# The last row block of a hybrid decoder layer: one group of 512 columns, and a bias that waits in the output

## The chip, the core and the metric

The kernel runs on one core of one Trainium2 chip. A core has TensorE (matrix products into PSUM), VectorE, ScalarE, GpSimd and SyncE, each with its own queue of instructions, and 16 DMA engines that all queues share. The metric is the device time of one execution in microseconds; the time before is the median of three runs.

## The reference

One decoder layer on 512 tokens of width 1024: two token mixers (a gated MLP and a differential attention) are projected, gated and merged, and the result goes through one more projection, a residual sum and a LayerNorm. What matters here is its end, cut to this:

```python
merged = jax.nn.sigmoid(ga) * (ya @ w_branch_a[i]) + jax.nn.sigmoid(gb) * (yb @ w_branch_b[i])
mix_out = merged @ w_out[i]
ple = jax.nn.sigmoid(x @ w_ple_gate[i]) * (p[i] @ w_ple[i])
x = layer_norm(DEEPNORM_ALPHA * x + mix_out + ple, ln_g[i], ln_b[i])
```

`layer_norm` takes mean and variance of each token's 1024 values, and returns (value - mean) * (variance + 1e-5)^-0.5 * ln_g + ln_b, in float32.

## The kernel before, in words

Every product is made of three passes (`three`): each float32 operand is split into a high and a low part, and high x high, high x low and low x high are added up in PSUM. `product` issues one pass and counts it; work on other engines is written out by hand with `later(n, ...)`, which puts a call n passes ahead, so that its instructions enter their engines' queues at that place. Each engine works through its queue in order. Tile semaphores are set by the framework; instructions wait only for what they read or overwrite.

The final projection works on four row blocks of 128 tokens (t = 0 to 3) and 1024 columns. A PSUM bank holds 128 x 512 float32. The first half of the columns (0 to 511) is done for row blocks 0 and 1 together, then 2 and 3; the second half row block by row block, t = 0 to 3, 8 slices of the contraction with three passes each. Before its products, a bank is filled by ScalarE (`fill`, L1321) with what is to be added: the gated embedding, and for the last row block also the residual, so that for t = 3 the finished sum stands in PSUM. For t < 3 the residual is added by VectorE in `stats` (L1338), into the SBUF tile `base`.

For the last row block alone, the second half is cut into two groups of 256 columns (`last_columns`, L1318), each in a bank of its own: 24 passes of 256 columns into a bank of tag `sc`, then 24 into one of tag `pp`. The statistics of the first group (`bn_stats`, L1341) run while TensorE does the second.

`last_norm` (L1343) normalizes a row block. `rstd_of` (L1091) lets VectorE aggregate the statistics (L1093) and add epsilon to the variance (L1094), and GpSimd raise it to the power -0.5 (L1096). Meanwhile VectorE centres: it subtracts the mean and multiplies by `ln_g` (L1351), for t = 3 straight from PSUM in three operations of 512, 256 and 256 columns. Then it scales by the power and adds `ln_b` (L1355), for t = 3 in two halves, and SyncE stores each half as it is finished (L1356).

Two queues matter beside these. SyncE issues the loads of the weights and, behind them, the stores of the output; its queue is empty between the last load and the first store. GpSimd issues the transfers that add to their destination (L324, L365, L1246). The last of them adds x to `base` for the last row block; behind it, in `later(RETIRE, pool.drain)` (L1382), GpSimd is told to drain. When all is issued, the program's end (L1435) drains each engine and lets them meet.

Of the kernel before, what the change touches and what calls it, by code (L numbers as in the profile page):

```python
# [17 lines left out]
AF = mybir.ActivationFunctionType  # L18
OP = mybir.AluOpType
AX = mybir.AxisListType  # L20

P = 128
D = 1024
T = 512
KT = D // P
NT = T // P
# [4 lines left out]
ALPHA = 2.0 ** 0.25  # L31
LAM_INIT = 0.2
EPS = 1e-5
# [52 lines left out]
MERGE = (36, 36, 25, 27), (40, 40, 68, 62)  # L86
RESIDUE = (176, 190, 204, 164)
FIRST_FILL = (150, 156)
FILL = ((14, 0, 1), (20, 2, 0), (24, 1, 1), (44, 3, 0), (110, 2, 1), (124, 3, 1), (150, 3, 2))
RETIRE = 8  # L90

# [135 lines left out]
def bcast(ap, n, parts=P):  # L229
    return bass.AP(tensor=ap.tensor, offset=ap.offset, ap=[[0, parts], [1, n]])  # L230
# [3 lines left out]
def hybrid_layer(ctx: ExitStack, tc: tile.TileContext, a, out: bass.AP):  # L234
    nc = tc.nc
    pe, dve, act, pool, sp = nc.tensor, nc.vector, nc.scalar, nc.gpsimd, nc.sync
# [12 lines left out]
    def pp():  # L249
        return pbank("pp", 3)  # L250
# [11 lines left out]
    def later(n, fn, *args):  # L262

        clock[1] += 1
        heapq.heappush(agenda, (clock[0] + n, clock[1], fn, args))

    def product(ps, s, m, start, stop, read_within=False):
        pe.matmul(ps, s, m, start=start, stop=stop, skip_group_check=read_within)  # L268
        clock[0] += 1
        while agenda and agenda[0][0] <= clock[0]:  # L270
            _, _, fn, args = heapq.heappop(agenda)
            fn(*args)
# [6 lines left out]
    def three(ps, s_h, s_l, m_h, m_l, first, last, read_within=False):  # L279

        product(ps, s_h, m_h, first, False, read_within)
        product(ps, s_h, m_l, False, False, read_within)
        product(ps, s_l, m_h, False, last, read_within)
# [3 lines left out]
    raw, split = {}, {}  # L287
    cursor = [0]

    def cut(h, l, x, alone=False):  # L290
        if alone:
            dve.tensor_copy(h, x)
        else:
            act.activation(h, x, AF.Copy)  # L294
        dve.tensor_tensor(out=l, in0=x, in1=h.bitcast(F32), op=OP.subtract)  # L295
# [37 lines left out]
    def load(u, cuts=(0, 1024), first=(sp,)):  # L333
        if u >= len(STEPS) or u in raw or STEPS[u][3] is not None:
            return
        _, unit, chain, _ = STEPS[u]
        if pumping:
            if not free:
                return
            home[u] = free.popleft()  # L340
            r = home[u]()
        elif chain == "a":
            r = sums[0]()
        else:
            ring.rotate(-1)
            home[u] = ring[-1]
            r = home[u]()
        raw[u] = r
        for j, s in enumerate(map(slice, cuts, cuts[1:])):
            queue = first[j] if j < len(first) else sp  # L350
            queue.dma_start(out=r[:, s], in_=weights(unit)[:, s])
            yield

    def follow(u):

        if u not in FOLLOWS:
            back = home.pop(u, None)
            if pumping and back:
                free.append(back)
                pump()  # L360
        else:
            raw[FOLLOWS[u]] = raw[u]
            if u in home:
                home[FOLLOWS[u]] = home.pop(u)
            pool.dma_start(out=raw[u], in_=weights(STEPS[FOLLOWS[u]][1]), accum_op=OP.add)  # L365

    def parts_of(u):
        h = wsp.tile([P, 1024], F32R, name="wh", tag="wh")
        l = wsp.tile([P, 1024], F32R, name="wl", tag="wl")
        split[u] = (h, l)  # L370
        return h, l

    def prep(u, cuts=(0, 1024)):
        if u < len(STEPS) and u not in split:
            run(load(u))
            h, l = parts_of(u)
            for s in map(slice, cuts, cuts[1:]):
                cut(h[:, s], l[:, s], raw[u][:, s])
                yield
            follow(u)  # L380
# [17 lines left out]
    def next_unit(name):  # L398
        u = cursor[0]
        assert STEPS[u][0] == name, (STEPS[u][0], name)  # L400
        cursor[0] += 1
        for g in (prep(u), prep(u + 1), prep(u + 2)):
            run(g)
        if not pumping:
            for v in range(u + 3, u + 6):
                run(load(v))
        spread(u + 3)
        if name in EARLY_ASK:
            later(ASK, lambda: run(load(u + 6)))
        return split.pop(u)  # L410
# [27 lines left out]
    def run(gen):  # L438
        for _ in gen:
            pass  # L440
# [24 lines left out]
    xh = big.tile([P, KT, T], F32R, name="xh", tag="X0")  # L465
    xl = big.tile([P, KT, T], F32R, name="xl", tag="X1")
# [6 lines left out]
    def ask_xr(k):  # L473
# [14 lines left out]
                       base=0, pattern=[[-1, P]], channel_multiplier=1)  # L488
    mhalf = consts.tile([P, 8], F32, name="mhalf")
# [4 lines left out]
    cs = rp.tile([P, T], F32, name="cs")  # L494
# [12 lines left out]
    def small(shape, name, bufs=6):  # L507
        return consts.tile(shape, F32, name=name, tag=name, bufs=bufs)
# [62 lines left out]
    cuts = [prep(u, halves) for u in range(3)]  # L571
# [43 lines left out]
    def of_sum(parts, c):  # L615
        def at(t, k):
            ts = slice(0, 2 * P) if t is None else slice(t * P, (t + 1) * P)
            return parts[0][:, c, k, ts], parts[1][:, c, k, ts]

        return at  # L620
# [313 lines left out]
    for k in range(KT):  # L934
        if k % 2 == 0:
            h, l = next_unit("kq")
# [93 lines left out]
    for g in range(KT):  # L1030
        bank = pp()
# [59 lines left out]
    def rstd_of(st):  # L1091
        mv = small([P, 2], "mv")
        dve.bn_aggr(out=mv, in_=st)  # L1093
        dve.tensor_scalar(out=mv[:, 1:2], in0=mv[:, 1:2], scalar1=EPS, scalar2=None, op0=OP.add)  # L1094
        rs = small([P, 1], "rs")
        pool.tensor_tensor(out=rs, in0=mv[:, 1:2], in1=mhalf[:, 0:1], op=OP.pow)  # L1096
        return mv, rs
# [110 lines left out]
    base = post.tile([P, NT, D], F32, name="base", tag="V")  # L1208
# [44 lines left out]
    for c in (1, 0):  # L1253
        h, l = next_unit("ple")
        for t in range(NT):
            ts = slice(t * P, (t + 1) * P)
            for k in range(2):
                m = slice(k * T, (k + 1) * T)
# [33 lines left out]
    norm_last = []  # L1292
# [13 lines left out]
    def merge_turn(c, t, m):  # L1306
        bank = pbank("tr" if t % 2 else "po", 1)
        for j in range(4):
# [6 lines left out]

    of_ya = (of_parts(xh, xl, 0, 0), of_parts(xh, xl, 4, 0), of_parts(xh, xl, 4, 2 * P),
             of_sum(ys, 2), of_sum(ys, 1), of_sum(ys, 0), of_apart)
    last_columns = [[(0, T), (T, D)] for _ in range(NT - 1)] + [[(0, T), (T, T + T // 2), (T + T // 2, D)]]  # L1318
    held = {}

    def fill(t, i):  # L1321
        c0, c1 = last_columns[t][i]
        bank = (pbank("sc", 2) if (t < 2 and i == 0) or (t >= 2 and i == 1) else
                pbank("tx", 1) if t == 2 else pp())
        held[t, i] = bank[:, :c1 - c0]
        act.activation(held[t, i], base[:, t, c0:c1], AF.Copy, scale=1.0 if t < NT - 1 else ALPHA)

    for t in range(2):
        later(FIRST_FILL[t], fill, t, 0)
# [10 lines left out]
            bank = z  # L1340
        dve.bn_stats(out=zst[t][:, piece, :], in_=bank)  # L1341

    def last_norm(t, cuts):  # L1343
        mv, rs = rstd_of(zst[t])
        lg, lb = norm_last
        if t < NT - 1:
            first = [(base[:, t, :], slice(0, D))]
        else:
            first = [(held[t, i], slice(*c)) for i, c in enumerate(last_columns[t])]
        for source, cs in first:  # L1350
            dve.scalar_tensor_tensor(out=base[:, t, cs], in0=source, scalar=mv[:, 0:1], in1=lg[:, cs],  # L1351
                                     op0=OP.subtract, op1=OP.mult)
        for cs in cuts:
            z = base[:, t, cs]
            dve.scalar_tensor_tensor(out=z, in0=z, scalar=rs[:, 0:1], in1=lb[:, cs], op0=OP.mult, op1=OP.add)  # L1355
            sp.dma_start(out=out[t * P:(t + 1) * P, cs], in_=z)  # L1356

    zst = [small([P, 2 if t < NT - 1 else 3, 6], "vst", 4) for t in range(NT)]
    units = []
    for n, t, i in FILL:  # L1360
        later(n, fill, t, i)
    for those in ((0, 1), (2, 3)):
        for k in range(KT):
# [9 lines left out]
            h, l = units[k // 2]  # L1373
            m = slice((k % 2) * T, (k % 2 + 1) * T)
            for t in those:
                ts = slice(t * P, (t + 1) * P)
# [4 lines left out]
    spread(cursor[0] + 3, *OUT_SECOND)  # L1381
    later(RETIRE, pool.drain)  # L1382
    units = []
    for t in range(NT):
        ts = slice(t * P, (t + 1) * P)
        for i, (c0, c1) in enumerate(last_columns[t][1:], 1):
            for k in range(KT):
                if len(units) <= k // 2:
                    run(prep(cursor[0]))
                    units.append(split.pop(cursor[0]))  # L1390
                    cursor[0] += 1
                h, l = units[k // 2]
                m = slice((k % 2) * T + c0 - T, (k % 2) * T + c1 - T)
                three(held[t, i], xh[:, k, ts], xl[:, k, ts], h[:, m], l[:, m], False, k == KT - 1, True)
            later(1, stats, t, i, held[t, i])
        later(1, last_norm, t, [slice(0, D)] if t < NT - 1 else [slice(0, T), slice(T, D)])
    flush()


# [39 lines left out]
```

## Time and profile before

| | us |
|---|---|
| median of 3 runs (lowest, highest) | 611.57 (611.23, 611.86) |
| the profiled execution | 611.03 |
| its span, first to last instruction | 609.3 |
| TensorE busy | 601.1 (99%) |
| VectorE busy | 466.3 (77%) |
| ScalarE busy | 345.9 (57%) |
| GpSimd busy | 125.1 (21%) |

The profile is one execution, and its times are counted from the start of its span. PE is TensorE, DVE VectorE, ACT ScalarE, POOL GpSimd and SP SyncE; a "q" behind the name means the engine's queue of issued instructions, such as DMA issues and drains. L and a number is the line of the kernel. The chain of work that ended last is followed back from the last instruction, at each step to what released it. The granted clock of TensorE was 0.996 of full speed.

### The profile page before, as it was taken

What the parts mean: (1) busy time and instruction counts of PE and PEld (TensorE: products, weight loads), DVE (VectorE), ACT (ScalarE), POOL (GpSimd) and SP (SyncE); (2) the same over time, 40 slices, a digit from 0 to 9 for tenths busy, and PEclk for the clock granted to TensorE, in tenths of its full rate; (3) what the DMA queues carried; (4) which work ended last, traced back from release to release, by engine and by line L of the source; (5) the groups of instructions that cost most, each with busy time, mean ns of one, the idle gap of its engine ahead of it and who ended that gap; (6) DMA issues with size and microseconds to landing.
All of it is one profiled execution on the core that took longest, in us unless ns stands there. A gap on an engine that the chain in (4) does not pass through costs nothing.

```text
span 609.3 us, 8273 instructions
## 1 busy us (share of the span) xinstructions
PE 601.1 (99%) x2880; PEld 501.9 (82%) x2880; DVE 466.3 (77%) x770; ACT 345.9 (57%) x537; POOL 125.1 (21%) x133
## 2 busy tenths in 40 slices
PE   9999999999999999999999999999999999999995
PEld 6888888888888888888888888888888888888885
DVE  6995645588789789777966779779687887879476
ACT  6656475754745745747576666554776565555310
POOL 1234121040350530520211322331120011110011
PEclk9999999999999999999999999999999999999998
DMA  8689899696886996893479988976999578998002
GB/s 307 226 248 183 251 206 224 238 252 237 276 196 249 308 248 243 220 317 108 118 305 294 291 245 215 267 186 185 287 242 312 173 202 251 239 248 308 31 35 103
DMA packets 44541, 138.23 MB, mean 227 GB/s; under 512 B 5940, under 2 KB 7092, under 8 KB 44148
## 3 DMA queue, kind: packets, MB, share of 16 engines
q1 hardware_dynamic: 34436, 102.97, 47.0%
q0 software_dynamic: 9488, 34.35, 30.8%
q8 instruction: 22, 0.36, 0.2%
q10 hardware_dynamic: 576, 0.39, 0.2%
q14 instruction: 19, 0.16, 0.1%
HBM read 118.69 MB, written 29.49 MB: 243 GB/s over the span
## 4 chain that ended last, share of the span: by engine, by line
PE 98%; DVE 1%; DMA 1%; DVEq 0%; issue 0%
PE ps_pp L268 56%; PE ps_sc L268 22%; PE ps_tx L268 9%; PE ps_sc L770 3%; PE ps_po L815 3%; PE ps_tr L804 1%; PE ps_po L268 1%; PE ps_tr L268 1%; PE ps_tr L1123 1%; PE ps_po L1123 1%; DMA xr<-in_xT 1%; PE ps_tx L858 1%; PE ps_tr L1309 0%; PE ps_po L1309 0%; DVE base L1351 0%; DVE xl L295 0%
## 5 line engine op out<-in xcount | busy, mean ns | idle before, releaser
L392 DVE TENSOR_TENSOR wl<-wr,wh 128x1024 fp32r<-128x1024 f32 x133 | 166.4, 1259 | 39.8 <-ACT wh L389 39.7
L389 ACT ACTIVATE wh<-wr 128x1024 fp32r<-128x1024 f32 x133 | 139.2, 1054 | 73.3 <-PE ps_pp L268 18.0
L268 PE MATMUL ps_pp<-xh,wh 128*128 128x512 f32 x232 | 94.0, 406 | 0.0
L268 PE MATMUL ps_pp<-xl,wh 128*128 128x512 f32 x232 | 92.7, 400 | 0.2 <-DVE xl L295 0.2
L268 PE MATMUL ps_pp<-xh,wl 128*128 128x512 f32 x232 | 91.8, 396 | 0.0
L783 ACT ACTIVATE p<-p,sth 128x128 f32<-128x128 f32 (+3 forms) x64 | 35.5, 556 | 41.1 <-DVE sth L781 41.1
L365 POOL DMA_DIRECT2D wr<-in_w x30 | 25.8, 873 | 155.8 <-DVE wl L392 152.8
L268 PE MATMUL ps_pp<-wl,xh 128*128 128x512 f32 (+1 forms) x148 | 56.9, 384 | 0.0
L268 PE MATMUL ps_pp<-wh,xl 128*128 128x512 f32 (+1 forms) x148 | 56.8, 384 | 0.0
L268 PE MATMUL ps_pp<-wh,xh 128*128 128x512 f32 (+1 forms) x148 | 56.7, 383 | 0.0
L268 PEld LDWEIGHTS ps_pp<-xl,wh 128*128 128x128 f32 x232 | 43.7, 188 | 7.9 <-DVE xl L295 0.5
L268 PEld LDWEIGHTS ps_pp<-xh,wh 128*128 128x128 f32 x232 | 43.7, 188 | 7.9 <-ACT wh L294 0.5
L268 PEld LDWEIGHTS ps_pp<-xh,wl 128*128 128x128 f32 x232 | 43.7, 188 | 7.7
L777 DVE CUSTOM_DVE_ANT_0 p<-ps_sc,mask 128x128 f32<-128x128 f32 (+3 forms) x64 | 31.0, 484 | 12.3 <-PE ps_sc L770 12.1
L715 POOL TENSOR_TENSOR hl<-m,hl 128x512 fp32r<-128x512 f32 x16 | 24.7, 1585 | 56.4 <-ACT hl L710 54.9
L268 PE MATMUL ps_sc<-wl,xsh 128*128 128x512 f32 x88 | 34.5, 392 | 0.0
L268 PE MATMUL ps_sc<-wh,xsh 128*128 128x512 f32 x88 | 34.4, 390 | 0.0
L268 PE MATMUL ps_sc<-wh,xsl 128*128 128x512 f32 x88 | 34.3, 390 | 0.0
L268 PEld LDWEIGHTS ps_pp<-wh,xh 128*128 128x128 f32 x148 | 27.8, 188 | 5.5
L268 PEld LDWEIGHTS ps_pp<-wl,xh 128*128 128x128 f32 x148 | 27.8, 188 | 5.4
L268 PEld LDWEIGHTS ps_pp<-wh,xl 128*128 128x128 f32 x148 | 27.8, 188 | 5.4
L268 PE MATMUL ps_pp<-wh,xsl 128*128 128x512 f32 x72 | 28.1, 390 | 0.0
(304 smaller groups left out, 1317.8 us busy)
## 6 DMA issues: line engine op xcount, KB each, us to landing
wr<-in_w SPq DMA_DIRECT2D x83, 512.0 KB, 5.4
wr<-in_w POOLq DMA_DIRECT2D x30, 512.0 KB, 7.2
wa<-in_w POOLq DMA_DIRECT2D x12, 512.0 KB, 6.5
k<-hl SPq DMA_DIRECT2D x16, 256.0 KB, 4.7
q<-hl SPq DMA_DIRECT2D x16, 256.0 KB, 4.3
ws_va<-in_w POOLq DMA_DIRECT2D x8, 512.0 KB, 9.8
wr<-ws_va SPq DMA_DIRECT2D x8, 512.0 KB, 4.8
kx<-hl SPq DMA_DIRECT2D x12, 256.0 KB, 6.3
```

What stands on the lines that cost most here:

```text
L268: pe.matmul(ps, s, m, start=start, stop=stop, skip_group_check=read_within)
L365: pool.dma_start(out=raw[u], in_=weights(STEPS[FOLLOWS[u]][1]), accum_op=OP.add)
L389: act.activation(h, raw[u], AF.Copy)
L392: dve.tensor_tensor(out=l, in0=raw[u], in1=h.bitcast(F32), op=OP.subtract)
L715: pool.tensor_tensor(out=hl[:, 3 - j, :], in0=m[2 * j], in1=hl[:, j, :].bitcast(F32), op=OP.subtract)
L770: pe.matmul(sc[m][:, :n], q[:, m, i * P:(i + 1) * P], kk[:, m, :n], start=o == 0, stop=o == 1)
L777: dve.tensor_tensor_reduce(out=pr[m][:, :n], in0=sc[m][:, :n], in1=mask[:, T - n:], scale=-(DK ** -0.5), scalar=3e38, op0=OP.add, op1=OP.m ...
L783: act.activation(pr[m][:, :n], pr[m][:, :n], AF.Exp, bias=st[:, m:m + 1], scale=-1.0, accum_out=st[:, 2 + m:3 + m])
L804: pe.transpose(tr[:, j * P:(j + 1) * P], ad[:, j * P:(j + 1) * P], ident)
L815: pe.matmul(po[:, i * P:(i + 1) * P], at[:, j * P:(j + 1) * P], v[:, j, h * P:(h + 1) * P], start=j == 0, stop=j == i)
L858: pe.transpose(tr[:, i * P:(i + 1) * P], on[:, i, :], ident)
L1123: pe.matmul(sa[:, t * P:(t + 1) * P], va[:, t, g * P:(g + 1) * P], aux[0][:, 0, g, :], start=True, stop=True)
```

## The change

The change concerns the last row block (t = 3), and nothing else.

- Its second half of the columns is one group of 512 again: 24 passes of 512 columns instead of 48 of 256, one fill, two pieces of statistics instead of three.
- Epsilon is added by ScalarE (an Identity with a bias per row) instead of VectorE; the power stays on GpSimd.
- VectorE centres two halves of 512 columns. The second half is scaled and shifted by VectorE and stored by SyncE as before.
- The first half is scaled by ScalarE, and not shifted. Instead, `shift_first` has SyncE write `ln_b` into the 128 rows and 512 columns of the output itself, from memory to memory, 100 passes into the final projection's count; and after the scaling GpSimd issues a transfer that adds the scaled half to what stands there.
- A constant of one column (`eps`) is set by GpSimd ahead of the projection.

`last_norm` is split into `centre` and `scale_and_shift`, which issue the same instructions as before for t < 3. The diff, with the parts that only take out the loop over groups cut:

```diff
-FILL = ((14, 0, 1), (20, 2, 0), (24, 1, 1), (44, 3, 0), (110, 2, 1), (124, 3, 1), (150, 3, 2))
+FILL = ((14, 0, 1), (20, 2, 0), (24, 1, 1), (44, 3, 0), (110, 2, 1), (124, 3, 1))
 RETIRE = 8
+SHIFT = 100
...
-    last_columns = [[(0, T), (T, D)] for _ in range(NT - 1)] + [[(0, T), (T, T + T // 2), (T + T // 2, D)]]
+    last_columns = [slice(0, T), slice(T, D)]
...
+    def centre(t, source, cs, mv):
+        dve.scalar_tensor_tensor(out=base[:, t, cs], in0=source, scalar=mv[:, 0:1], in1=norm_last[0][:, cs],
+                                 op0=OP.subtract, op1=OP.mult)
+
+    def scale_and_shift(t, cs, rs):
+        z = base[:, t, cs]
+        dve.scalar_tensor_tensor(out=z, in0=z, scalar=rs[:, 0:1], in1=norm_last[1][:, cs],
+                                 op0=OP.mult, op1=OP.add)
+        sp.dma_start(out=out[t * P:(t + 1) * P, cs], in_=z)
+
+    def last_norm(t):
         if t < NT - 1:
...
+            mv, rs = rstd_of(zst[t])
+            centre(t, base[:, t, :], slice(0, D), mv)
+            scale_and_shift(t, slice(0, D), rs)
+            return
+        mv, var, rs = (small([P, n], name) for n, name in ((2, "mv"), (1, "var"), (1, "rs")))
+        dve.bn_aggr(out=mv, in_=zst[t])
+        act.activation(var, mv[:, 1:2], AF.Identity, bias=eps[:, 0:1])
+        pool.tensor_tensor(out=rs, in0=var, in1=mhalf[:, 0:1], op=OP.pow)
+        for i, cs in enumerate(last_columns):
+            centre(t, held[t, i], cs, mv)
+        z = base[:, t, last_columns[0]]
+        act.activation(z, z, AF.Copy, scale=rs[:, 0:1])
+        pool.dma_start(out=out[t * P:(t + 1) * P, last_columns[0]], in_=z, accum_op=OP.add)
+        scale_and_shift(t, last_columns[1], rs)
+
+    def shift_first():
+        sp.dma_start(out=out[T - P:T, 0:T], in_=bcast(a["ln_b"], T))
+
+    eps = small([P, 1], "eps", 1)
+    pool.memset(eps, EPS)
+    later(SHIFT, shift_first)
+    zst = [small([P, 2, 6], "vst", 4) for t in range(NT)]
```

More of the change, by code (lines that the diff above doesn't have):

```diff
@@ L1317, in hybrid_layer @@
              of_sum(ys, 2), of_sum(ys, 1), of_sum(ys, 0), of_apart)
-    last_columns = [[(0, T), (T, D)] for _ in range(NT - 1)] + [[(0, T), (T, T + T // 2), (T + T // 2, D)]]
+    last_columns = [slice(0, T), slice(T, D)]
     held = {}
     def fill(t, i):
-        c0, c1 = last_columns[t][i]
         bank = (pbank("sc", 2) if (t < 2 and i == 0) or (t >= 2 and i == 1) else
                 pbank("tx", 1) if t == 2 else pp())
-        held[t, i] = bank[:, :c1 - c0]
-        act.activation(held[t, i], base[:, t, c0:c1], AF.Copy, scale=1.0 if t < NT - 1 else ALPHA)
+        held[t, i] = bank
+        act.activation(held[t, i], base[:, t, last_columns[i]], AF.Copy, scale=1.0 if t < NT - 1 else ALPHA)
     for t in range(2):
@@ L1341, in stats @@
         dve.bn_stats(out=zst[t][:, piece, :], in_=bank)
-    def last_norm(t, cuts):
-        mv, rs = rstd_of(zst[t])
-        lg, lb = norm_last
-        if t < NT - 1:
[L1347 to L1356, printed above, removed]
@@ L1358, in hybrid_layer @@
-    zst = [small([P, 2 if t < NT - 1 else 3, 6], "vst", 4) for t in range(NT)]
+    def centre(t, source, cs, mv):
[6 more added lines that the diff above has]
+        sp.dma_start(out=out[t * P:(t + 1) * P, cs], in_=z)
@@ L1385, in hybrid_layer @@
         ts = slice(t * P, (t + 1) * P)
[L1386 to L1396, printed above, removed]
+        for k in range(KT):
+            if len(units) <= k // 2:
+                run(prep(cursor[0]))
+                units.append(split.pop(cursor[0]))
+                cursor[0] += 1
+            h, l = units[k // 2]
+            m = slice((k % 2) * T, (k % 2 + 1) * T)
+            three(held[t, 1], xh[:, k, ts], xl[:, k, ts], h[:, m], l[:, m], False, k == KT - 1, True)
+        later(1, stats, t, 1, held[t, 1])
+        later(1, last_norm, t)
     flush()
```

## The prediction

> **What bounds the kernel now.** I read the page first, then the chain of work that ended last from 560 us on, then the timeline of the last 8 us, then the store that ends last.
>
> ```profile
> span 609.3 us, 8273 instructions
> ...
> PE 98%; DVE 1%; DMA 1%; DVEq 0%; issue 0%
> ```
>
> TensorE carries 98% of the chain. The change takes no work from it but in the last row block, so everything is decided in the last 18 us. The chain there (start, us, what):
>
> ```profile
> 579.79 11.56 PE ps_pp L268 x51
> 591.35 8.31 PE ps_sc L268 x48
> 599.66 2.89 PE ps_pp L268 x24
> ...
> 602.58 0.44 DVE vst L1341
> ...
> 603.04 0.25 DVE mv L1093
> ...
> 603.32 0.15 DVE mv L1094
> 603.47 0.72 DVE base L1351 x2
> ...
> 604.44 0.47 DVE base L1351
> 604.91 0.66 DVE base L1355
> 605.57 0.66 DVEq L1435
> ```
>
> The last product ends at 602.55. From there the chain is all VectorE: the statistics of the last 256 columns, the aggregate, adding epsilon, three centring operations (512, 256 and 256 columns), two scale-and-shifts. The timeline gives those operations their own durations, and GpSimd's power beside them:
>
> ```profile
> 603.39 0.74 DVE L1351 SCALAR_TENSOR_TENSOR base<-ps_pp,mv,ln_g 128x512 f32<-128x512 f32 x1
> 603.55 0.54 POOL L1096 TENSOR_TENSOR rs<-mv,mhalf 128x1 f32<-128x1 f32 x1 [3.20 <-DVE mv L1094]
> 604.04 0.47 DVE L1351 SCALAR_TENSOR_TENSOR base<-ps_sc,mv,ln_g 128x256 f32<-128x256 f32 x1
> ...
> 604.83 1.40 DVE L1355 SCALAR_TENSOR_TENSOR base<-base,rs,ln_b 128x512 f32<-128x512 f32 x2
> ```
>
> Power is done at 604.09 and waits for nobody; VectorE isn't ready to use it before 604.83. The last store (issue, its time to landing) and SyncE's first drain after it:
>
> ```profile
> L1356 SPq DMA_DIRECT2D out<-base x1: 332/332/332, 606.3 to 606.3; - x1
> ```
> ```profile
> out<-base SPq DMA_DIRECT2D x1, 256.0 KB, 2.0
> ```
> ```profile
> L1435 SPq DRAIN  x1: 13/13/13, 608.4 to 608.4; - x1
> ```
>
> So the last bytes land at 606.3 + 2.0 = 608.3, SyncE drains at 608.4, and the span ends at 609.3: 1.0 us of closing after the landing. The sum below is against this span. The execution took 611.03 us as a whole, 1.73 more than its span, and the median of the three runs, 611.57, is another 0.54 higher; I add the difference of spans to the median. About 0.2% (1.2 us) is what a measurement of this kernel can tell from no change.
>
> **Part by part: up to the centring.** Products: the 51 of 512 columns took 11.56 us, 0.227 each, so 24 take 5.44. Of the 8.31 us of ps_sc the first 24 are row block 2's (5.44), which leaves 2.87 for 24 of 256 columns; with the 2.89 of ps_pp the two groups take 5.76. One group of 512 saves 0.32: the last product ends at 602.23. Against that, half the statistics were done while the second group ran; now all 512 columns come behind the last product.
>
> ```profile
> 582.75 0.69 DVE L1341 BATCH_NORM_STATS2 vst<-ps_pp 128x6 f32<-128x512 f32 x1
> ...
> 598.36 0.21 DVE L1093 BATCH_NORM_AGGREGATE mv<-vst 128x2 f32<-128x12 f32 x1
> ```
>
> Statistics 0.69 for 0.43 (+0.26), the aggregate over two pieces 0.21 for 0.25 (-0.04). The aggregate ended at 603.29; now at 603.29 - 0.32 + 0.26 - 0.04 = 603.19. Nearly the whole gain of the products is given back to the statistics.
>
> **VectorE after it.** The epsilon addition (0.15) leaves VectorE, so centring starts 0.15 earlier, at 603.24. Operations of 512 columns follow each other by 0.65 (603.39 to 604.04) and take 0.74: the second centring runs 603.89 to 604.63, the one scale-and-shift left from 604.55 (it overlaps by 0.08, as in the rows) to 605.29. Its store goes out at 605.36 instead of 606.3 and lands at 607.36, 0.94 earlier than the last store of before. That would be the gain if it were still last.
>
> **The other half: ScalarE, GpSimd, accumulating transfer.** Epsilon goes to ScalarE on one column, and the scaling of 512 columns with a scale read per row. Nearest rows: two columns, 512 columns from SBUF to SBUF, and 512 columns with a per-row operand (busy, mean ns):
>
> ```profile
> L595 ACT ACTIVATE lame<-lamd 128x2 f32<-128x2 f32 x1 | 0.2, 204 | 0.0
> ...
> L1211 ACT ACTIVATE base<-base 128x512 f32<-128x512 f32 x4 | 2.5, 623 | 0.9 <-DVE base L641 0.8
> ...
> L859 ACT ACTIVATE yb<-ps_tx,g 128x512 f32<-128x512 f32 x7 | 4.8, 682 | 2.8 <-PE ps_tx L858 2.8
> ```
>
> A hand-over costs 0.08 (603.47, end of epsilon, to 603.55, start of power). ScalarE starts at 603.27, ends at 603.47; power runs 603.55 to 604.09, just where it was: the extra hand-over and the slower addition eat the 0.10 by which the aggregate is earlier. The first half was centred by 603.98, so scaling waits for power: 604.17 to 604.82 (0.65, between 0.62 and 0.68). Nothing is queued behind it on ScalarE, whose last instruction of before is this fill:
>
> ```profile
> 586.67 0.39 ACT L1326 ACTIVATE ps_pp<-base 128x256 f32<-128x256 f32 x1 [4.31 <-DVE base L1338]
> ```
>
> GpSimd starts to issue at 604.90.
>
> Power stays at 0.54 only because centring reads PSUM. In row block 2, where centring has both large inputs in SBUF, power lasts until 0.4 after it:
>
> ```profile
> 598.67 1.27 DVE L1351 SCALAR_TENSOR_TENSOR base<-base,mv,ln_g 128x1024 f32<-128x1024 f32 x1
> ...
> 598.84 1.51 POOL L1096 TENSOR_TENSOR rs<-mv,mhalf 128x1 f32<-128x1 f32 x1 [4.00 <-DVE mv L1094]
> ```
>
> The new scale-and-shift has both in SBUF and runs until 605.29, beside the issue on GpSimd. If the issue is held as power is, it loses up to 0.4; at the least, nothing.
>
> The transfer decides. The trace has no accumulating transfer of 256 KB out of SBUF on idle queues; the nearest is one of 512 KB from memory to memory at 290 us with the other queues quiet (issue, time to landing, and the DMA share, last column but one, and GB/s around its start and end):
>
> ```profile
> 290.45 0.89 POOL L324 DMA_DIRECT2D ws_ga<-in_w  x1 [0.20 <-ACT wh L389]
> ```
> ```profile
> ws_ga<-in_w POOLq DMA_DIRECT2D x1, 512.0 KB, 5.2
> ```
> ```profile
> 291.75:292.00 0.25, 0.25 (x4) 0.17 (x2) 0.25 (x1) 0.07 (x1) 0.25 (x1) 1.00 0.00 0
> 292.00:292.25 0.25, 0.25 (x5) 0.25 (x3) 0.25 (x1) 0.00 (x0) 0.25 (x1) 1.00 2.14 229
> 294.75:295.00 0.25, 0.25 (x2) 0.19 (x1) 0.25 (x1) 0.00 (x0) 0.00 (x0) 1.00 0.53 115
> 295.00:295.25 0.25, 0.25 (x2) 0.19 (x1) 0.25 (x2) 0.00 (x0) 0.00 (x0) 1.00 0.05 0
> ```
>
> From 290.45 to the first packets 1.55 us, packets for 3.0, then 0.65 to the landing: 5.2. Half the bytes: 1.55 + 1.5 + 0.65 = 3.7. Bounds: at the plain rate the packets take half of that, and at the full 3.0, if time goes by rows and not by bytes (128 rows both times), it stays 5.2. The two queues' lines on the page give the plain rate:
>
> ```profile
> q1 hardware_dynamic: 34436, 102.97, 47.0%
> q0 software_dynamic: 9488, 34.35, 30.8%
> ```
>
> q1 moves 102.97 MB in 0.47 of 609.3 us, 360 GB/s; q0, nearly all accumulating, 34.35 MB in 0.308, 183 GB/s. So 256 KB plain take 0.73 and the lower bound is 1.55 + 0.73 + 0.65 = 2.9. I take 3.7, as the byte rates of the two queues differ by the two that an accumulation reads. Beside the other half's store, in flight until 607.36, it may lose up to 0.7; I add 0.2, since only their ends overlap. Landing: 604.9 + 3.7 + 0.2 = 608.8, against 608.3. With the closing of 1.0 the span is 609.8, +0.5: 611.57 + 0.5 = 612.1 us.
>
> Here the Trainium skill has a rule ("DMA: Bandwidth & Descriptors", Anatomy of one DMA): a transfer issued from GpSimd costs about 2.0 us plus its bytes at 436 GB/s. The row at 290 us differs: 512 KB would be 3.2 by it, and took 5.2. By the page as an estimate 256 KB take 2.6, the landing is at 607.5 and the sum is 0.8 below before, 610.8 us.
>
> **The bias put into the output.** SyncE has no wait before it and nothing behind it but the four row blocks' stores. It reaches the first of these at 558.1, and the DMA engines are quiet from about 566 to 590 (40 slices of 1.25 us from 560 on):
>
> ```profile
> L1356 SPq EVENT_SEMAPHORE  x5: 17/17/28, 558.1 to 606.0; - x5
> ```
> ```profile
> DMA  9997000000000000000000000720036000900820
> ```
>
> It goes out near 558 behind the last weights of its queue and lands in the quiet stretch: nothing. Without that cover it would cost its 0.73 on the engines. The fill left out and the constant set on GpSimd after its last load have idle engines: nothing.
>
> **The rivals.** *GpSimd's closing drain, slower.* Before the change GpSimd drains early, right behind its last transfer:
>
> ```profile
> 537.89 1.20 POOL L1246 DMA_DIRECT2D base<-in_x  x1
> ```
> ```profile
> base<-in_x POOLq DMA_DIRECT2D x1, 512.0 KB, 11.9
> ```
> ```profile
> L272 POOLq DRAIN  x1: 14848/14848/14848, 537.8 to 537.8; - x1
> ```
>
> The transfer landed at 549.8; the drain ended at 537.8 + 14.85 = 552.65, 2.85 later. Now a transfer follows that drain, and the closing one waits for it. If it always outlasts the landing by 2.85, GpSimd is done at 611.65; from SyncE's drain the end took 0.9: 612.55, +3.25, 614.8 us. It decides as soon as it outlasts the landing by the 0.1 after which SyncE drains. For it: a drain has never been seen cheap behind an open transfer. Against: that one stood behind all of q0's transfers, 69 of them (65 of 512 KB and 4 of 64 KB make the 34.35 MB); if it goes by their number, one costs 0.04, and DMA was busy until 565. If it counts from the issue (13.6 after GpSimd's instruction), the span ends at 620.2, 622.5 us.
>
> Here too the Trainium skill differs: "VectorE: DVE Perf Modes", The DRAIN you can't avoid, puts the drains of a program's end at some 12 ns on all engines; by that this rival costs nothing. The 14,848 ns show that it doesn't hold behind an open transfer.
>
> *Time by rows.* The transfer takes 5.2: landing at 610.3, +2.0, 613.6 us. For it: rows of 2 KB instead of 4. Against: the byte rates above.
>
> *Plain price.* The transfer takes 2.9, landing at 607.8, -0.5, 611.1 us. VectorE's store at 607.36 is next, so even free accumulation gives 0.94 at most: the change can't be faster by 1.2 us unless something unseen goes.
>
> **How the numbers follow.** Forecast 0.65, on its own 611.5 to 612.8 (issue and overlap give 0 to 0.9 more than the bare landing, handing-over some 0.3 less); plain price 0.09; time by rows 0.10; drain 0.14, and 0.02 for its long form. Slower by over 0.2%: drain 0.16, rows 0.10, and 0.04 of the forecast where holding and overlap come together: 0.30. Faster: 0.02 of the plain price. Same: 0.68. The range, 611.2 to 615.0, takes in the forecast, rows and the short drain; it leaves out the plain price and the long drain.
>
> **What would show it.** Last product 0.3 earlier; one statistics row of 0.69 behind it; power ending near 604.1; ScalarE's scaling ending at 604.8; GpSimd's issue at 604.9 and 3.9 to landing; SyncE's store landing at 607.4; a closing drain of GpSimd that ends 0.1 after the landing. Wrong if that drain ends microseconds later, if the landing takes over 4.4 or under 3.2, or if power lasts 1.5.

## The result, and the profile after

The changed kernel takes 612.88 us (median of 22 executions, 612.36 to 619.74) against 611.46 before (22, 610.87 to 612.16). The ratio of the two, taken within rounds of executions, is 1.0032 (95% interval 1.0019 to 1.0044): slower, by 0.3%. The quotient of the medians is 1.0023; both lie in the interval. The forecast of 612.1 was 0.5 over before where 1.4 was measured; the time lies in the range and just above the forecast's own range, which ended at 612.8.

The profiled execution has a span of 612.8 us, 3.5 more than before, and not all of that is the change's. The chain that ended last, at the row that answers to the first of before (row blocks 0 and 1, second half), starts at 581.56 instead of 579.79:

```profile
581.56 11.56 PE ps_pp L269 x51
593.12 5.45 PE ps_sc L269 x24
```

So 1.77 us more had gone by when this row began (more on that below), and 1.73 are lost from there on. I call the stretch from this row to the end of the span the last part: 29.5 us before, 31.2 after. The timeline of the last row block:

```profile
604.04 0.70 DVE L1341 BATCH_NORM_STATS2 vst<-ps_sc 128x6 f32<-128x512 f32 x1 [0.60 <-PE ps_sc L269]
604.77 0.21 DVE L1360 BATCH_NORM_AGGREGATE mv<-vst 128x2 f32<-128x12 f32 x1
605.02 0.75 DVE L1344 SCALAR_TENSOR_TENSOR base<-ps_pp,mv,ln_g 128x512 f32<-128x512 f32 x1
605.08 0.29 ACT L1361 ACTIVATE var<-mv,eps 128x1 f32<-128x1 f32 x1 [20.73 <-DVE mv L1360]
605.45 0.55 POOL L1362 TENSOR_TENSOR rs<-var,mhalf 128x1 f32<-128x1 f32 x1 [3.33 <-ACT var L1361]
...
606.03 0.72 ACT L1366 ACTIVATE base<-base,rs 128x512 f32<-128x512 f32 x1 [0.66 <-POOL rs L1362]
606.53 0.75 DVE L1349 SCALAR_TENSOR_TENSOR base<-base,rs,ln_b 128x512 f32<-128x512 f32 x1
607.05 0.92 POOL L1367 DMA_DIRECT2D out<-base  x1 [1.05 <-ACT base L1366]
```

Less 1.77, these are times of before. The aggregate ends at 603.21 and centring starts at 603.25, as forecast to 0.02. Power is ready at 604.23, 0.14 late, of which 0.09 is ScalarE's 0.29 for one column; scaling ends at 604.98. Then comes a hand-over of 0.30 (606.75 to 607.05), almost four times what I had taken, and GpSimd issues at 605.28. This isn't the hold by VectorE that the prediction had as a condition: in the trace of before, GpSimd's transfers start as long after the VectorE operation that they wait for, 0.29 both beside an operation with its inputs in SBUF (353.07 to 353.36) and with VectorE idle (404.13 to 404.42). The transfers out of that part, with their time to landing:

```profile
out<-base POOLq DMA_DIRECT2D x1, 256.0 KB, 4.4
out<-base SPq DMA_DIRECT2D x1, 256.0 KB, 2.0
```

VectorE's scaling starts 0.10 after the centring that it needs, not 0.08 ahead of its end, so it ends at 605.51 in times of before and SyncE's store lands at 607.5 (607.36 forecast); the adding transfer at 607.05 + 4.4 = 611.45, which is 609.7 in times of before against the 608.8 of the forecast. What follows the landing, by the instructions of the program's end (durations in ns, first and last start in us; 611.45 to 611.95):

```profile
L1452 SPq EVENT_SEMAPHORE  x8: 28/28/3707, 607.8 to 611.9; - x8
L1452 POOLq DRAIN  x1: 4499/4499/4499, 607.0 to 607.0; - x1
L1452 SPq DRAIN  x1: 13/13/13, 611.9 to 611.9; - x1
```

and in the profile before, from 607.65 to 608.45:

```profile
L1435 SPq EVENT_SEMAPHORE  x3: 28/28/28, 607.6 to 608.4; - x3
L1435 SPq DRAIN  x1: 13/13/13, 608.4 to 608.4; - x1
```

GpSimd's drain ends at 607.0 + 4.5 = 611.5, with the landing. But SyncE passes nine semaphores one by one ahead of its own drain (ten before). It now stands at the second from 607.8 on for 3.7 us, and has seven to walk through when it is released; before, two were left after 607.65, and it passed them at 608.3 and 608.4, after the last landing. Its drain comes 0.45 after the landing instead of 0.1, and the span ends 1.35 after it instead of 1.0.

### The profile page after: what moved, and what is told of

Its sections match the earlier page's. It is cut to its first block, busy times and chain, and to the rows that moved or that the text cites. A ratio compares the mean times of both kernels' runs of the same rounds, so it can differ in the third digit from the quotient of the medians.

```text
span 612.8 us, 8227 instructions
## 1 busy us (share of the span) xinstructions
PE 601.8 (98%) x2856; PEld 500.5 (82%) x2856; DVE 465.7 (76%) x766; ACT 346.5 (57%) x538; POOL 126.3 (21%) x135
## 3 DMA queue, kind: packets, MB, share of 16 engines
q0 software_dynamic: 9632, 34.61, 31.3%
## 4 chain that ended last, share of the span: by engine, by line
PE 88%; issue 7%; DMA 2%; DVE 1%; POOL 0%; ACT 0%; POOLq 0%; DVEq 0%; ACTq 0%
PE ps_pp L269 50%; PE ps_sc L269 18%; PE ps_tx L269 6%; PE ps_sc L771 3%; PE ps_po L816 3%; DMA wr<-in_w 2%; PE ps_tr L805 1%; PE ps_po L269 1%; PE ps_tr L269 1%; PE ps_po L463 1%; PE ps_tr L1124 1%; PE ps_po L1124 1%; DMA wr<-ws_wb 1%; PE ps_tx L859 0%; DVE wl L393 0%
## 5 line engine op out<-in xcount | busy, mean ns | idle before, releaser
L269 PE MATMUL ps_pp<-wl,xh 128*128 128x512 f32 x140 | 54.6, 390 | 0.0
L269 PE MATMUL ps_pp<-wh,xl 128*128 128x512 f32 x140 | 54.6, 390 | 0.0
L269 PE MATMUL ps_pp<-wh,xh 128*128 128x512 f32 x140 | 54.5, 389 | 0.0
L269 PEld LDWEIGHTS ps_pp<-wl,xh 128*128 128x128 f32 x140 | 26.3, 188 | 5.4
L269 PEld LDWEIGHTS ps_pp<-wh,xh 128*128 128x128 f32 x140 | 26.3, 188 | 5.4
L269 PEld LDWEIGHTS ps_pp<-wh,xl 128*128 128x128 f32 x140 | 26.3, 188 | 5.4
L269 PE MATMUL ps_sc<-wl,xh 128*128 128x512 f32 x72 | 28.3, 393 | 0.5 <-DVE wl L393 0.5
```

## The experiments

Each kernel is the changed one with the edit shown, if nothing else is said. The table has all of them; the last part is the end of the span less the start of the chain's row of 51 products, from one profile each (for the two kernels that were profiled twice it differs by 0.3 and 0.1). An interval that doesn't hold 1 is a difference from before.

| kernel | ratio to before (95% interval) | row of 51 starts | span | last part |
|---|---|---|---|---|
| before | | 579.79 | 609.3 | 29.5 |
| changed | 1.0032 (1.0019 to 1.0044) | 581.56 | 612.8 | 31.2 |
| again | 1.0011 (1.0002 to 1.0020) | 579.48 | 610.4 | 30.9 |
| plain_pool | 0.9996 (0.9987 to 1.0004) | 579.57 | 609.3 | 29.7 |
| plain_sp | 0.9983 (0.9974 to 0.9992) | 580.53 | 609.4 | 28.9 |
| one_group | 0.9982 (0.9973 to 0.9991) | 579.40 | 608.7 | 29.3 |
| one_group_again | 0.9989 (0.9980 to 0.9998) | 580.27 | 609.5 | 29.2 |
| no_drain | 1.0056 (1.0043 to 1.0068) | 579.99 | 613.4 | 33.4 |
| half_bytes | 1.0013 (1.0004 to 1.0022) | 580.28 | 610.6 | 30.3 |
| no_bias | 1.0019 (1.0011 to 1.0028) | 579.69 | 610.7 | 31.0 |
| interleaved | 0.9996 (0.9987 to 1.0005) | 579.56 | 609.1 | 29.5 |
| eps_scalar | 0.9991 (0.9982 to 1.0000) | 579.82 | 609.0 | 29.2 |
| two_groups | 1.0037 (1.0023 to 1.0050) | 581.25 | 612.5 | 31.3 |
| alone | one execution, no ratio | 580.90 | 611.4 | 30.5 |

**again**, the same kernel, no edit.

> The changed kernel once more. Tail theory (all the loss lies behind the last product: the transfer is issued late, takes 4.4 us instead of 2.0, and the closing walk takes 1.35 instead of 1.0): median 1.4 us over before, last product to the end of the span 8.8 us (6.75 before), whatever the rest of the execution does. Upstream theory (the 1.77 us by which the changed kernel's profile reached the last transposes later, 561.74 for 559.98, belong to the change as well): the last transposes again near 561.7, and the median 3 us over before.

```profile
579.48 11.56 PE ps_pp L269 x51
```
```profile
out<-base POOLq DMA_DIRECT2D x1, 256.0 KB, 4.1
```

The same program comes to this row 2.1 us earlier than in its first profile. So the 1.77 are not the change's, and the upstream theory falls; the row starts anywhere between 579.4 and 581.6 in these fourteen profiles. The spans of all executions say the same: their median, less the last part of the profile, puts the row's start at about 580.0 for the changed kernel (22 executions), 579.8 here (11), 580.0 to 580.3 for before (27, 33 and 22) and 579.7 to 580.5 for the other timed kernels. The first profile of the changed kernel had caught a late start.

The last part is 1.4 longer than before (1.7 in the first profile; 0.3 of that difference is the landing). By medians the time is 0.8 us over before (611.62 here), where 1.4 were expected and measured the first time; the two intervals meet at 1.0019 to 1.0020, somewhat under the 0.23% to 0.28% that the last part alone makes.

**plain_pool.**

```diff
-        pool.dma_start(out=out[t * P:(t + 1) * P, last_columns[0]], in_=z, accum_op=OP.add)
+        pool.dma_start(out=out[t * P:(t + 1) * P, last_columns[0]], in_=z)
```

> The transfer of the first half stays on GpSimd's queue but overwrites instead of adding, so the bias is missing there. Tail theory: 2.9 us from issue to landing instead of 4.4, so 1.5 us less than the changed kernel, the same as before within 0.3 us; the closing walk stays at 1.35. Rival (the queue is what costs, not the addition): 4 us or more to landing and still 1 us over before.

```profile
out<-base POOLq DMA_DIRECT2D x1, 256.0 KB, 3.0
```

3.0 to landing, and the last part is 29.7: the addition itself costs 1.1 to 1.4 us, as the tail theory has it, and without it the change would just about break even.

**plain_sp.**

```diff
-        pool.dma_start(out=out[t * P:(t + 1) * P, last_columns[0]], in_=z, accum_op=OP.add)
+        sp.dma_start(out=out[t * P:(t + 1) * P, last_columns[0]], in_=z)
```

> The first half, scaled by ScalarE, is stored by SyncE without adding; the bias is missing there, and no transfer is issued by GpSimd after its drain. Tail theory: both stores land near 607.4 and 606.8 in the times of before, the closing walk is back at 1.0, and the kernel is 0.5 to 0.9 us faster than before. Upstream theory: it stays over before by the 1.5 us that have nothing to do with the tail.

```profile
604.99 0.72 ACT L1366 ACTIVATE base<-base,rs 128x512 f32<-128x512 f32 x1 [0.66 <-POOL rs L1362]
...
605.74 0.33 SPq L1367 DMA_DIRECT2D out<-base  x1
606.27 0.33 SPq L1351 DMA_DIRECT2D out<-base  x1
```

SyncE issues 0.03 after ScalarE's end, where GpSimd needed 0.30. The last part is 28.9, 0.6 less than before, and the time 1.0 less. This is what the whole change would gain if the bias came for nothing; 0.2 to 0.3 of the 0.6 are the one group's (next run), so ScalarE's share is 0.3 to 0.4. GpSimd's queue and the addition then cost 2.0 to 2.4 us of the last part.

**one_group** and **one_group_again**, the same kernel twice: only the group of 512 columns is kept.

```diff
-        mv, var, rs = (small([P, n], name) for n, name in ((2, "mv"), (1, "var"), (1, "rs")))
...
+        mv, rs = rstd_of(zst[t])
         for i, cs in enumerate(last_columns):
             centre(t, held[t, i], cs, mv)
...
+        for cs in last_columns:
+            scale_and_shift(t, cs, rs)
```

> Only the group of 512 columns is kept; epsilon, scaling, bias and stores of the last row block are VectorE's and SyncE's as before. Sum of the prediction: 0.32 less of products, 0.26 more of statistics, 0.04 less of the aggregate, one centring less: 0.2 us faster, same within the measurement. Rival (the two half groups hid the statistics and were worth more): 0.3 us slower or more.

> The one-group kernel once more. In its first run the time was 0.9 us less than before while its profile's last part was only 0.2 us shorter. Tail theory: the last part is 0.2 us shorter again, and the time comes out 0.2 to 0.8 us less than before. Rival (the one group is worth 0.9 us somewhere outside the last part): 0.9 us less again, with the last part 0.2 shorter.

```profile
602.92 0.74 DVE L1344 SCALAR_TENSOR_TENSOR base<-ps_pp,mv,ln_g 128x512 f32<-128x512 f32 x1
603.58 0.74 DVE L1344 SCALAR_TENSOR_TENSOR base<-ps_sc,mv,ln_g 128x512 f32<-128x512 f32 x1
604.24 1.40 DVE L1349 SCALAR_TENSOR_TENSOR base<-base,rs,ln_b 128x512 f32<-128x512 f32 x2
```

The last part is 0.2 and 0.3 shorter than before, the predicted sum. The times are 0.9 and 0.5 us less than before (medians), 0.1% to 0.2%, and both intervals lie below 1: this is the version with the full result that beats both kernels. The median span is 0.70 and 0.35 shorter than before; what the first pair gains beyond the last part isn't explained by it.

**no_drain.**

```diff
-    later(RETIRE, pool.drain)
```

> The changed kernel without GpSimd's early drain, so that the closing drain stands behind all 70 transfers of its queue. If a drain's time behind the landing goes by the number of transfers since the last drain (2.85 us for 69 before), the closing drain ends 2.8 us after the landing and the kernel is 2.5 us slower than the changed one. If the 2.85 came from the busy DMA engines of that moment, the closing drain still ends 0.1 after the landing and nothing changes.

The transfer and the closing drain:

```profile
out<-base POOLq DMA_DIRECT2D x1, 256.0 KB, 4.2
```
```profile
L1451 POOLq DRAIN  x1: 7115/7115/7115, 605.5 to 605.5; - x1
```

Issued at 605.48, landed at 609.7; the drain ends at 605.5 + 7.1 = 612.6, 2.9 later, with the DMA engines idle. The last part is 33.4, 2.2 to 2.5 more than with the early drain. So the 2.85 us don't come from traffic: the first drain pays them, behind 69 transfers when it stands early and behind 70 here, and a second drain behind one transfer costs about nothing. Whether they go by the number of transfers or come with the first drain whatever the number, no run here tells apart.

**half_bytes.** The other 256 columns of the half are left at the bias.

```diff
-        pool.dma_start(out=out[t * P:(t + 1) * P, last_columns[0]], in_=z, accum_op=OP.add)
+        pool.dma_start(out=out[t * P:(t + 1) * P, 0:T // 2], in_=z[:, 0:T // 2], accum_op=OP.add)
```

> The adding transfer takes only the first 256 of its 512 columns: 128 rows of 1 KB instead of 2 KB; the other 256 columns stay at the bias. If time goes by bytes, 3.1 to 3.3 us from issue to landing instead of 4.1 to 4.4; if it goes by rows, no less than 4.0. Tail theory: what the landing gains the time gains, so 1.0 us less than the changed kernel with bytes and nothing with rows.

```profile
out<-base POOLq DMA_DIRECT2D x1, 128.0 KB, 3.5
```

Between the two: half the bytes save 0.6 to 0.9 of 4.1 to 4.4. Neither the rule by bytes (3.1 to 3.3) nor the one by rows (4.0) is met. The first packets come 1.9 after the issue, as with the whole half, and they run for 1.3 instead of 1.9 to 2.1.

**no_bias.** The sum in the last half is made with what stands in the output.

```diff
-    later(SHIFT, shift_first)
```

> The changed kernel without the store that puts the bias into the output; the transfer adds to what stands there. The prediction put that store at nothing: within 0.3 us of the changed kernel, the part up to row block 2's products where it is in other executions (579 to 582). Rival (the store delays the last weights or rows): 0.5 us or more less than the changed kernel, all of it ahead of the last row block.

The last part is 31.0 with a landing after 4.2, and the ratio lies between those of the two runs of the changed kernel. No cost of the store of the bias shows, as predicted: it goes out at 559.8 in the changed kernel and lands 8.3 later, in the quiet stretch.

**interleaved**, from the one-group kernel:

```diff
-        for i, cs in enumerate(last_columns):
-            centre(t, held[t, i], cs, mv)
-        for cs in last_columns:
+        centre(t, held[t, 0], last_columns[0], mv)
+        scale_and_shift(t, last_columns[0], rs)
+        centre(t, held[t, 1], last_columns[1], mv)
+        for cs in (slice(T, D - P), slice(D - P, D)):
             scale_and_shift(t, cs, rs)
```

> One group of 512 columns, everything else on VectorE and SyncE as before, but in another order: the first half is centred, scaled and stored before the second is centred, and the second half is scaled and stored as 384 and 128 columns. From the one-group kernel's rows: VectorE ends at the same place or 0.1 later, the last store is 64 KB and lands in 1.4 to 1.5 instead of 2.0: last product to the end of the span 6.3 to 6.5 us (6.75 before, 6.85 with one group); 0.2 to 0.5 us faster than the one-group kernel. Rival (the stores queue up behind each other on the DMA engines): no change from the one-group kernel.

```profile
603.09 0.74 DVE L1344 SCALAR_TENSOR_TENSOR base<-ps_pp,mv,ln_g 128x512 f32<-128x512 f32 x1
603.93 0.75 DVE L1349 SCALAR_TENSOR_TENSOR base<-base,rs,ln_b 128x512 f32<-128x512 f32 x1
604.60 0.74 DVE L1344 SCALAR_TENSOR_TENSOR base<-ps_sc,mv,ln_g 128x512 f32<-128x512 f32 x1
605.38 0.88 DVE L1349 SCALAR_TENSOR_TENSOR base<-base,rs,ln_b 128x384 f32<-128x384 f32 x2
```
```profile
out<-base SPq DMA_DIRECT2D x1, 192.0 KB, 2.0
out<-base SPq DMA_DIRECT2D x1, 64.0 KB, 1.8
```

My idea fails twice. An operation that needs the one before it starts 0.78 to 0.84 after that one's start, where independent ones follow by 0.66 (one_group's rows): VectorE ends 0.46 later, counted from the row of 51. And the small store lands only 1.8 after its issue behind the larger one. The last part is 0.2 to 0.3 longer than the one-group kernel's.

**eps_scalar**, from the one-group kernel:

```diff
-        mv, rs = rstd_of(zst[t])
+        mv, var, rs = (small([P, n], name) for n, name in ((2, "mv"), (1, "var"), (1, "rs")))
+        dve.bn_aggr(out=mv, in_=zst[t])
+        act.activation(var, mv[:, 1:2], AF.Identity, bias=eps[:, 0:1])
+        pool.tensor_tensor(out=rs, in0=var, in1=mhalf[:, 0:1], op=OP.pow)
```

> The one-group kernel with epsilon added by ScalarE, as in the change; scaling, bias and stores stay on VectorE and SyncE. From the rows: centring starts 0.15 earlier, power is ready 0.28 later and still before the second centring ends, so the last store is 0.15 earlier: the last part 0.15 shorter than the one-group kernel's. Rival (power becomes late): no shorter, with VectorE waiting for power.

```profile
603.27 0.75 DVE L1344 SCALAR_TENSOR_TENSOR base<-ps_pp,mv,ln_g 128x512 f32<-128x512 f32 x1
```

Centring starts 23.45 after the start of the row of 51; in one_group it is 602.92 - 579.40 = 23.52. Moving epsilon gains 0.07, not 0.15: in one_group, too, centring started before the addition had run to its end. The last part is the same as one_group's within 0.1.

**two_groups**: the kernel before, with ScalarE, the bias in the output and the adding transfer as in the change.

```diff
+            if t == NT - 1 and i == 0:
+                act.activation(z, z, AF.Copy, scale=rs[:, 0:1])
+                pool.dma_start(out=out[t * P:(t + 1) * P, cs], in_=z, accum_op=OP.add)
+                continue
```

> The other half of the change alone: two groups of 256 columns as before, and ScalarE, the waiting bias and the adding transfer as in the change. If the parts add up (one group 0.2 less, whole change 1.4 to 1.7 more in the last part), 1.6 to 1.9 us more than before in the last part. Rival (the one group is what makes the transfer late): 1 us more or less.

The last part is 1.7 longer than before, with 4.4 to landing. With the 0.2 to 0.3 that one group saves, 1.5 are left, between the 1.4 and 1.7 measured for the whole: the parts add up.

**alone.** The second half of the last row block isn't stored.

```diff
-        scale_and_shift(t, last_columns[1], rs)
+        z = base[:, t, last_columns[1]]
+        dve.scalar_tensor_tensor(out=z, in0=z, scalar=rs[:, 0:1], in1=norm_last[1][:, last_columns[1]],
+                                 op0=OP.mult, op1=OP.add)
```

> The changed kernel without SyncE's store of the last row block's second half, so the adding transfer has the DMA engines to itself; those columns are not written. If sharing the engines with that store made the first packet late and the transfer long: first packet 1.55 us after the issue, 3.7 to landing. If the transfer needs that long by itself: 1.9 and 4.1 to 4.4 again.

```profile
out<-base POOLq DMA_DIRECT2D x1, 256.0 KB, 3.7
```

Without the store beside it the transfer lands after the 3.7 that the prediction had for the bare transfer. The packets of the changed kernel show how the store gets in its way. From 608.0 to 608.9 only SyncE's queue has packets, from 609.0 to 611.2 only GpSimd's (packets, MB, share of the 16 engines):

```profile
q1 hardware_dynamic: 137, 0.26, 79.4%
```
```profile
q0 software_dynamic: 139, 0.25, 82.9%
```

The adding transfer's first packets come 1.9 us after its issue, as the store's are done, instead of 1.5 alone (607.86, after the issue at 606.38). That is 0.4, all of what the second profile lost to the store (4.1 for 3.7). The first profile lost 0.3 more while its packets ran (2.1 us, with the store's already done; 1.8 alone, 1.9 to 2.0 in again, no_bias and no_drain); why is open.

## Why the prediction was right, and where it was off

The place and the mechanism were right: what VectorE's path gained (its store lands at 607.5, 0.8 earlier) is not worth anything, as the adding transfer ends last. The step that failed is its landing: "Landing: 604.9 + 3.7 + 0.2 = 608.8". Measured are 609.7 (609.4 in the second profile). Two terms of this sum were too small, and so was the closing behind it.

- **The issue**: 605.28 instead of 604.90. The 0.08 from one operation to the next on another engine doesn't hold for a transfer issued from GpSimd (0.30); ScalarE took 0.29 and 0.72 for 0.20 and 0.65. Together +0.38. The hold of up to 0.4 by VectorE, the forecast's condition for a late issue, didn't happen.
- **The store beside it**: taken at 0.2 of a bound of 0.7. The transfer took 4.1 to 4.4, and 3.7 alone: 0.4 to 0.7. "Only their ends overlap" was the wrong reason: the store's packets came just where the first of the adding transfer were due. The 3.7 itself stood, in part by luck: alone, the packets ran 0.3 longer than the 1.5 of the sum (607.86 to 609.68), and the landing came 0.4 behind them instead of 0.65.
- **The closing**: "the closing of 1.0" is no constant. It was 1.35, for SyncE waits for this transfer ahead of others and has their semaphores still to pass. It goes by the transfer that lands last: plain_pool, with GpSimd's last, has 1.2 from landing to end; plain_sp, with SyncE's last, 1.0.

0.38 + 0.5 + 0.35 on top of the predicted 0.5 make the 1.73 of the first profile. Each is small, all have the same sign, and together they carry the time past the 0.2%, while "same" had been given 0.68. Of the forecast itself only 0.04 went to more than 0.2% slower, for a hold at the issue that meets the store; what met was a longer hand-over, the store and the closing. The range holds the time by luck: its part above 612.8 was there for the rows and the drain, and neither happened.

The products, the statistics and the aggregate came out at the predicted sum (one_group: 0.2 to 0.3 less). Power at 0.55, VectorE's path (to 0.2) and the bias without a visible cost came out as told. One slip: epsilon was worth 0.07 and not 0.15, and the 0.10 by which the aggregate was earlier was left out of centring's start; they cancel to 0.02.

The drain, my rival on the slow side, is answered both ways. With the early drain kept, the closing one ended with the landing, within 0.1, so that rival wasn't it. But its 2.85 are real, and no_drain brings them back where no drain stands earlier. The rule of the Trainium skill ("VectorE: DVE Perf Modes", The DRAIN you can't avoid), some 12 ns, is for drains that the runtime puts ahead of and behind a program. SyncE's 13 ns here agree with it; GpSimd's 4,499 and 7,115 ns behind an open transfer don't, but all of these stand on the kernel's last line and needn't be the drains that it means. The early drain of 14,848 ns, which the prediction set against the rule, is the kernel's own instruction, so it says nothing on it. Time by rows alone and the plain price didn't happen either: half_bytes lies between rows and bytes, and plain_pool's 3.0 shows what the plain price would have been. The Trainium skill's sum for a transfer from GpSimd ("DMA: Bandwidth & Descriptors", Anatomy of one DMA), as an estimate 2.6 us for these bytes, is 0.4 under plain_pool's 3.0, which shared the engines with the store; for the adding transfer, 3.7 alone, it is 1.1 short.

What stays open: why one_group's time in its first run lies 0.7 us further below before than its last part explains. Its spans put 0.5 of this inside the span; the rest lies outside, where 7 of the 33 executions of before beside it spend 2.0 to 3.1 us and one_group's at most 1.8. In one_group_again only 0.05 is left inside, so it isn't shown to be the kernel's. The start of the last part varies by 2 us from profile to profile, for the same program too, and no run here tells the cause.

## What to carry to other kernels

Work that is moved to an idle engine at the end of a program brings that engine's way to the memory along: here ScalarE saved VectorE one operation of 0.7 us, and its result then took a path of GpSimd's issue, an addition on the way and the wait for another store's packets, and landed 2 us after VectorE's half. Price such a path to the last landing and on through the closing, with what lands beside it, and not to the end of the computing. Where GpSimd issues transfers through a program, a drain placed early in a quiet stretch can shorten the end: here it took 2.2 to 2.5 us off the last part.

## What the runs showed of the hardware that was not expected

- An adding transfer of 128 rows out of SBUF into memory takes 3.7 us for 256 KB alone (one execution) and 4.1 to 4.4 beside a store of the same size; 3.5 for 128 KB beside it; the plain one takes 3.0 beside it.
- GpSimd starts to issue a transfer 0.30 after ScalarE's end (0.29 after VectorE's), SyncE 0.03 after ScalarE's.
- GpSimd's closing drain ends within 0.1 us of the last landing with one transfer since the early drain, and 2.9 after it with 70 transfers and no drain before.
- SyncE passes the semaphores of the program's end one after the other, some 0.06 us each (seven from 611.5 to 611.9); a transfer that is awaited second of nine and lands last cost 0.35 more than one that was awaited last but one.
